# Hybrid decoder layer, S5 stage: one product with the B table, the state rotated ahead of one product with the C table, impulse-response products in four column groups

## The chip, the cores and the metric

The kernel runs on one core of one Trainium2 chip. The metric is the time of one execution on the device, in microseconds (us); lower is better. A core has five engines that matter here: TensorE (PE: products and transposes, the only one that writes sums to PSUM), VectorE (DVE), ScalarE (ACT), GpSimd (POOL) and SyncE (SP, which here only issues DMAs). Each engine takes its instructions in the order in which they were written to its queue; waits between engines go over semaphores.

## The reference

One decoder layer for a sequence of 1024 tokens with 1024 channels, all in float32: a token-mixing part with two branches (RWKV-7 and S5), merged by learned gates, an output projection, and a gated MLP with a short causal convolution. The change touches only the S5 branch, a diagonal complex state-space model over 32 groups of 16 channels with 64 complex states each:

```python
lam = lax.complex(a_re, a_im);  dt = jnp.exp(log_step)[:, None]
a_bar = jnp.exp(lam * dt)
b_bar = ((a_bar - 1.0) / lam)[..., None] * lax.complex(b_re, b_im)
bu = jnp.einsum('gpc,blgc->blgp', b_bar, ug)
_, states = lax.associative_scan(s5_combine, (a_elems, bu), axis=1)   # s_t = a_bar * s_(t-1) + bu_t
y = jnp.real(jnp.einsum('gcp,blgp->blgc', c, states)) + d * ug
y = jax.nn.gelu(y)
return y * jax.nn.sigmoid(y @ w_glu + b_glu)
```

## The kernel before

**Overall.** The front half of the kernel has three phases. First the norm and the projection of the S5 input u. Then the S5 stage. Then the RWKV stage, with merges and output projections. The MLP follows. Large products are made in three parts each (lines 172 to 174), since both operands are split into a high and a low float32r part; the three products for one block of 128 of the contracted dimension are one *step*, and eight steps make one 128 x 512 output of the input projection.

**S5 in blocks of eight tokens.** Eight tokens times 16 channels fill the 128 partitions, so a group's input is a 128 x 128 tile (`u8[b][:, g]`: one column for each block of eight tokens). A batch `b` is eight groups; there are four. Real parts of the 64 states lie in the partitions `HALF[0]` (0 to 63) and imaginary parts in `HALF[1]` (64 to 127). For a batch, `s5_tables` builds:
- `w` (lines 521 to 527), transposed on PE (546) and copied by ACT into `wT`: the B table, with a third block of 64 columns that is the negated first one (548);
- `ca`, the C table for nine powers (529 to 537), and `cb`, the same with its halves swapped and one negated (538, 539);
- `toep`, the direct part inside a block: products of B and C (`bb`, `ca`, line 555) give the impulse response, ACT copies it into `kpad` (556), DVE adds the skip term D (561), and eight DMAs spread it (564);
- `cs` and `sn`, cosines and sines of the rotation per block (566 to 577), and `ph`, the decay per block (578).

`s5_batch` then makes two sets of eight products with the B table, columns 0 to 127 and 64 to 191 of `wT` (599), so that the second set is the first one with its halves swapped and one of them negated. DVE rotates (602 to 604), scans over the blocks with real decay (605), and multiplies the scanned state `z` with `sn` and with `cs` (606, 607). Then come 24 products into one tile of PSUM: `toep` with u8, `ca` with `z*cs`, `cb` with `z*sn` (612 to 614). ACT copies the result out (615) and a DMA stores it in `YU` (616).

**What sets the order.** On PE the order is written out by a planner, `drive` (185). It has lanes, generators that emit PE instructions and yield a pair: the PE time of what they have emitted, and the time until their next part may run (or a condition). In the S5 stage there are two lanes, `s5_lane` for the batches and `tab_lane` for the tables; a batch needs its table, and table b needs batch b - 2. While no lane is due, or while the lanes have used more than their share of time (`PACE`, `CREDIT`), the planner emits *filler*: one step of the list `self.fill`, at 0.68 of its microseconds. Due times are constants (line 1907): `T_US` 5, `T_TAB` 20, `T_TRIG` 12, and `T_SCAN` 13 from the B products to the output products. The list holds the rest of the input projection (`mix_in`), the 16 gate tiles (`gate_tiles`), and later the merges (`merge`, `merge_s5`) and the output projection (`outproj`). When the S5 lanes are done, filler runs on until no accumulation is open (1834), and the RWKV lanes start (1848); the first half's outputs (`rwkv_out`, 924) put the merges on the list (1904). The other engines' queues are ordered by a scheduler of the language by priorities: filler above the S5 batches, these above the tables.

**Buffers.** The S5 products use the PSUM tile `chk` (two buffers), the filler `gm` (four buffers in the S5 stage, two in the RWKV stage). Tiles of 128 x 1024 that both functions share have the tag `T4` (eight buffers).

Of the kernel before, what the change touches and what calls it, by code (L numbers as in the profile page):

```python
# [9 lines left out]
F32 = mybir.dt.float32  # L10
# [3 lines left out]
ALU = mybir.AluOpType  # L14
# [11 lines left out]
HALF = (slice(0, 64), slice(64, 128))  # L26
# [40 lines left out]
class Kern:  # L67
# [425 lines left out]
    def s5_tables(self, b, d):  # L493

        nc, V, G, A = self.nc, self.nc.vector, self.nc.gpsimd, self.nc.scalar
        s, a = self.s5, self.a
        g8 = slice(b * 8, b * 8 + 8)
        mm = nc.tensor.matmul

        def bc_c(x):  # L500
            return x[:, g8].unsqueeze(2).to_broadcast([128, 8, 16])

        bre, bim, cre, cim = self.s5w[b]

# [24 lines left out]
        ca = self.s5p.tile([128, 8, 9, 16], F32, tag="ca", name=self.nm("ca"), bufs=2)  # L529
        ct = self.s5p.tile([128, 8, 9, 16], F32, tag="ct", name=self.nm("ct"))  # L530
        cb = self.s5p.tile([128, 8, 9, 16], F32, tag="cb", name=self.nm("cb"), bufs=2)
        def tab(eng, t, x, q, j0):
            eng.tensor_tensor(t[:, :, j0:9, :].rearrange("p g j c -> p j g c"), x.unsqueeze(1).to_broadcast([128, 9 - j0, 8, 16]),
                              q[:, j0:9, g8].unsqueeze(3).to_broadcast([128, 9 - j0, 8, 16]), ALU.mult)
        tab(V, ca, cre, s["q1"], 0)
        tab(V, ct, cim, s["q2"], 0)
        V.tensor_tensor(ca, ca, ct, ALU.add)
        A.copy(cb[HALF[0], :, 1:9, :], ca[HALF[1], :, 1:9, :])
        A.mul(cb[HALF[1], :, 1:9, :], ca[HALF[0], :, 1:9, :], -1.0)

        yield 0, T_TAB if b else T_TAB0

        wT = self.s5p.tile([128, 8, 3, 64], F32, tag="wT", name=self.nm("wT"))
        ps = self.chk().rearrange("p (g n) -> p g n", n=128)
        for g in range(8):
            nc.tensor.transpose(ps[:, g], w[:, g], self.cst("ident"))
        A.copy(wT[:, :, 0:2, :], ps.rearrange("p g (a n) -> p g a n", n=64))
        A.mul(wT[:, :, 2, :], ps[:, :, 0:64], -1.0)
        yield 1.0, 0

        kpad = self.s5p.tile([16, 8, 15, 16], F32, tag="kpad", name=self.nm("kpad"))
        G.memset(kpad[:, :, 0:7, :], 0.0)
        ps = self.chk().rearrange("p (g n) -> p g n", n=128)
        for g in range(8):
            mm(ps[0:16, g], bb[:, g, :], ca[:, g, 0:8, :], start=g % 4 == 0, stop=True, skip_group_check=True)
        A.copy(kpad[:, :, 7:15, :], ps[0:16].rearrange("p g (j c) -> p g j c", c=16))
        dg = self.s5p.tile([16, 8, 16], F32, tag="dg", name=self.nm("dg"))
        o, _ = CST["ident"]
        V.tensor_tensor(dg, self.csts[0:16, o:o + 16].unsqueeze(1).to_broadcast([16, 8, 16]),
                        s["d"][:, g8].unsqueeze(2).to_broadcast([16, 8, 16]), ALU.mult)  # L560
        V.tensor_tensor(kpad[:, :, 7, :], kpad[:, :, 7, :], dg, ALU.add)
        toep = self.t4(shape=(128, 8, 8, 16))
        for i in range(8):
            nc.sync.dma_start(toep[16 * i:16 * i + 16], kpad[:, :, i:i + 8, :])

        cs, sn, ph = self.t4(shape=(128, 8, 128)), self.t4(shape=(128, 8, 128)), self.t4(shape=(128, 8, 128))
        for t, f in ((ph, s["fh"]), (sn, s["fl"])):
            for g in range(8):
                A.activation(t[:, g], self.cst("nrow"), AF.Identity, scale=f[:, b * 8 + g:b * 8 + g + 1])
        V.tensor_scalar(cs, ph, MAGIC, -MAGIC, ALU.add, ALU.add)  # L570
        V.tensor_tensor(ph, ph, cs, ALU.subtract)
        V.tensor_tensor(ph, ph, sn, ALU.add)
        V.tensor_scalar(cs, ph, MAGIC, -MAGIC, ALU.add, ALU.add)
        V.tensor_tensor(ph, ph, cs, ALU.subtract)
        A.activation(cs, ph, AF.Abs)
        A.activation(sn, ph, AF.Sin, scale=SIN_SCALE)
        A.activation(cs, cs, AF.Sin, bias=self.hpi, scale=-SIN_SCALE)
        A.copy(ph, s["rho"][:, g8].unsqueeze(2).to_broadcast([128, 8, 128]))
        G.memset(ph[:, :, 0:1], 0.0)

        d.update(ca=ca, cb=cb, cs=cs, sn=sn, toep=toep, wT=wT, ph=ph)
        yield 1.8, T_TRIG

    def s5_batch(self, b, d, ys):

        nc, V, G, A = self.nc, self.nc.vector, self.nc.gpsimd, self.nc.scalar
        s = self.s5
        mm = nc.tensor.matmul
        ca, cb, cs, sn, toep, wT, ph = (d[n] for n in ("ca", "cb", "cs", "sn", "toep", "wT", "ph"))

        u8 = self.u8[b]
        z = self.t4(shape=(128, 8, 128))
        rot = self.t4(shape=(128, 8, 128))
        G.memset(rot[:, :, 0:1], 0.0)
        yield 0, T_US
        p1, p2 = (self.chk().rearrange("p (g n) -> p g n", n=128) for _ in range(2))
        for p, o in ((p1, 0), (p2, 1)):
            for g in range(8):
                mm(p[:, g], wT[:, g, o:o + 2, :], u8[:, g, :], start=g % 4 == 0, stop=True, skip_group_check=True)
        r2 = self.t4(shape=(128, 8, 128))  # L600
        lead, turn = (slice(None), slice(None), slice(0, 127)), rot[:, :, 1:128]
        V.tensor_tensor(turn, p1[lead], cs[lead], ALU.mult)
        V.tensor_tensor(r2[lead], p2[lead], sn[lead], ALU.mult)
        V.tensor_tensor(turn, turn, r2[lead], ALU.add)
        V.tensor_tensor_scan(*(t.rearrange("p g n -> p (g n)") for t in (z, ph, rot)), 0.0, ALU.mult, ALU.add)
        V.tensor_tensor(rot, z, sn, ALU.mult)
        V.tensor_tensor(z, z, cs, ALU.mult)
        y8 = self.t4(shape=(128, 8, 128))
        yield 3.6, T_SCAN
        ps = self.chk().rearrange("p (g n) -> p g n", n=128)  # L610
        for g in range(8):
            mm(ps[:, g], toep[:, g], u8[:, g, :], start=g % 4 == 0, stop=False, skip_group_check=True)
            mm(ps[:, g], ca[:, g, 1:9, :], z[:, g, :], start=False, stop=False, skip_group_check=True)
            mm(ps[:, g], cb[:, g, 1:9, :], rot[:, g, :], start=False, stop=True, skip_group_check=True)
        A.copy(y8, ps)
        nc.sync.dma_start(ys.rearrange("j c g n -> (j c) g n"), y8)
        yield 5.4, 0

# [1285 lines left out]
                self.fill += [self.merge(mg), self.merge_s5(self.first), self.outproj(0, mg, self.mx0)]  # L1904


T_US, T_TAB0, T_TAB, T_TRIG, T_SCAN = 5.0, 44.0, 20.0, 12.0, 13.0
T_LD, T_SQ, T_LT = 6.0, 3.0, 3.5
NEVA = 4
T_KN, T_BK, T_GR, T_NF, T_MT, T_INV, T_LV, T_CH = 7.0, 4.0, 4.0, 5.0, 8.0, 43.0, 1.0, 0.8  # L1910
# [86 lines left out]
```

## Time and profile before

| what | value |
|---|---|
| median of three runs | 1490.96 us (1488.9 to 1493.81) |
| span of the profiled execution (the page gives no other time for it) | 1491.1 us |
| PE busy, share of the span | 1435.8 us, 96% |
| PE weight loads | 1176.3 us, 79% |
| DVE busy | 1071.2 us, 72% |
| ACT busy | 729.8 us, 49% |
| first and last B product (line 599) | 131.0 and 241.6 us |
| last output product of S5 (line 614) starts | 260.6 us |

A busy time is the union of an engine's instructions; the ends of products are modelled, so what a set of products costs on PE is best read from the start of its first to the start of what follows. A row of the timeline gives start, duration, engine, line, operation, and in brackets the idle time before it with what ended it. A row of a table of stretches gives start and end, length, busy time and number of instructions for each engine, the granted clock of PE, and the DMA share and rate. A row of a group gives line, engine, operation, tiles, shapes and count, then busy time and the mean in ns, then idle time before it; where one line of the source is asked for, it gives shortest, median and longest in ns and the first and last start.

### The profile page before, as it was taken

The page shows a single profiled execution, that of the slowest core. Times are in us where ns is not written, and L with a number is a line of the kernel's source. Part 1 is how long each engine was busy: PE and PEld are TensorE (multiplying, and loading weights), DVE is VectorE, ACT ScalarE, POOL GpSimd, SP SyncE. Part 2 cuts the span into 40 slices and gives each one's busy share as a digit, 9 for nine tenths or more (in the row PEclk, how much of TensorE's full clock was granted, in tenths as well). Part 3 has the DMA queues.
Part 4 walks back from the last instruction along what each step waited for, and adds up shares of the span by engine and source line. Part 5 has one row for each costly group of instructions (what it writes and reads, how often), then busy time and mean ns, then how long its engine had stood idle before and what let it go on. Part 6 is the DMA issues. An engine that isn't in the chain of part 4 may idle for free. (4 is left out here: it accounts for less than half of the span.)

```text
span 1491.1 us, 24155 instructions
## 1 busy us (share of the span) xinstructions
PE 1435.8 (96%) x9284; PEld 1176.3 (79%) x9284; DVE 1071.2 (72%) x1761; ACT 729.8 (49%) x1167; POOL 58.9 (4%) x116
## 2 busy tenths in 40 slices
PE   7999999999999989899999999999999999999996
PEld 5778888778878778677878877888888887888785
DVE  8977765665325859646597798777777777697677
ACT  7677653443324553633554455444444444443351
POOL 0000000010100110100000000000000000000001
PEclk9999999999999999899999999999999999999998
DMA  6453433633511575733374643222222227934723
GB/s 217 121 194 116 129 94 91 212 113 122 164 59 58 171 226 163 189 109 108 121 222 150 205 127 121 85 85 85 85 85 81 76 70 260 328 125 133 236 83 113
DMA packets 121284, 206.26 MB, mean 138 GB/s; under 512 B 29248, under 2 KB 35520, under 8 KB 121168
## 3 DMA queue, kind: packets, MB, share of 16 engines
q1 hardware_dynamic: 113296, 182.43, 39.2%
q0 software_dynamic: 6144, 19.99, 4.0%
q10 hardware_dynamic: 1728, 2.29, 0.4%
q8 instruction: 73, 1.20, 0.4%
q14 instruction: 43, 0.35, 0.1%
HBM read 150.14 MB, written 52.43 MB: 136 GB/s over the span
## 5 line engine op out<-in xcount | busy, mean ns | idle before, releaser
L172 PE MATMUL gm<-hh,wh 128*128 128x512 f32 x672 | 277.0, 412 | 10.5 <-DVE ev L1192 4.3
L173 PE MATMUL gm<-hl,wh 128*128 128x512 f32 x672 | 265.4, 395 | 0.0
L174 PE MATMUL gm<-hh,wl 128*128 128x512 f32 x672 | 265.2, 395 | 0.0
L156 ACT CAST wh<-wf 128x512 fp32r<-128x512 f32 x171 | 105.6, 619 | 168.3 <-PE gm L173 103.8
L157 DVE TENSOR_TENSOR wl<-wf,wh 128x512 fp32r<-128x512 f32 x171 | 116.9, 686 | 77.6 <-ACT wh L156 77.3
L172 PEld LDWEIGHTS gm<-hh,wh 128*128 128x128 f32 x672 | 127.6, 190 | 42.8 <-issue 5.9
L174 PEld LDWEIGHTS gm<-hh,wl 128*128 128x128 f32 x672 | 128.0, 190 | 28.1
L173 PEld LDWEIGHTS gm<-hl,wh 128*128 128x128 f32 x672 | 128.2, 191 | 24.7 <-issue 1.0
L1615 PE MATMUL d<-xl,wh 128*128 128x512 f32 x308 | 121.4, 394 | 3.5 <-DVE xl L227 3.5
L1614 PE MATMUL d<-xh,wh 128*128 128x512 f32 x308 | 121.4, 394 | 2.1 <-ACT xh L226 2.1
L1616 PE MATMUL d<-xh,wl 128*128 128x512 f32 x308 | 121.2, 393 | 0.0
L1440 PE MATMUL rp<-t,h 128*128 128x512 f32 x216 | 84.4, 391 | 1.6 <-ACT p L1454 1.6
L1442 PE MATMUL rp<-t,l 128*128 128x512 f32 x216 | 84.2, 390 | 0.5 <-DVE l L227 0.5
L1441 PE MATMUL rp<-t,h 128*128 128x512 f32 x216 | 84.1, 389 | 0.0
L1615 PEld LDWEIGHTS d<-xl,wh 128*128 128x128 f32 x308 | 58.6, 190 | 16.5 <-DVE xl L227 4.3
L1614 PEld LDWEIGHTS d<-xh,wh 128*128 128x128 f32 x308 | 58.5, 190 | 14.8 <-ACT xh L226 2.5
L1616 PEld LDWEIGHTS d<-xh,wl 128*128 128x128 f32 x308 | 58.6, 190 | 12.2
L226 ACT CAST h<-r 128x1024 fp32r<-128x1024 f32 x34 | 35.8, 1054 | 61.1 <-PE rp L1441 29.6
L227 DVE TENSOR_TENSOR l<-r,h 128x1024 fp32r<-128x1024 f32 x34 | 41.6, 1224 | 29.2 <-ACT h L226 27.7
L1461 DVE SCALAR_TENSOR_TENSOR y<-zv,vecs,y 128x1023 f32<-128x1023 f32 (+1 forms) x36 | 46.1, 1280 | 8.5 <-ACT y L1459 8.5
L1440 PEld LDWEIGHTS rp<-t,h 128*128 128x128 f32 x216 | 40.5, 188 | 11.2 <-ACT p L1454 2.5
L1454 ACT COPY p<-rp 128x512 f32<-128x512 f32 x54 | 31.0, 574 | 36.5 <-PE rp L1442 36.5
(459 smaller groups left out, 3199.4 us busy)
## 6 DMA issues: line engine op xcount, KB each, us to landing
r<-in_w_up_dram SPq DMA_DIRECT2D x36, 512.0 KB, 3.7
wf<-in_w_in_dram SPq DMA_DIRECT2D x62, 256.0 KB, 3.1
st<-in_w_down_dram SPq DMA_DIRECT2D x55, 256.0 KB, 4.1
st<-ACT SPq DMA_DIRECT2D x44, 256.0 KB, 4.5
wf<-in_w_up_dram SPq DMA_DIRECT2D x36, 256.0 KB, 2.9
ACT<-y POOLq DMA_DIRECT2D x18, 512.0 KB, 2.9
GT<-ev SPq DMA_DIRECT2D x32, 256.0 KB, 2.6
wf<-in_w_br_dram SPq DMA_DIRECT2D x32, 256.0 KB, 2.9
```

Of the source, the lines that this page charges most:

```text
L156: nc.scalar.copy(h[:, :n], f[:, :n])
L157: nc.vector.tensor_tensor(l[:, :n], f[:, :n], h[:, :n].bitcast(F32), ALU.subtract)
L172: mm(ps, a, xh[k], start=k == 0, stop=False)
L173: mm(ps, a, xl[k], start=False, stop=False)
L174: mm(ps, b, xh[k], start=False, stop=k == n - 1)
L1440: mm(ps, wh[:, c], xh, start=first and k == 0, stop=False, skip_group_check=True)
L1441: mm(ps, wh[:, c], xl, start=False, stop=False, skip_group_check=True)
L1442: mm(ps, wl[:, c], xh, start=False, stop=k == 3, skip_group_check=True)
L1461: V.scalar_tensor_tensor(y[:, lag:], z[:, 0:1024 - lag], self.vec(nme, i), y[:, lag:], ALU.mult, ALU.add)
L1614: mm(ps, wh[:, c], xh[:, x], start=start, stop=False, skip_group_check=True)
L1615: mm(ps, wh[:, c], xl[:, x], start=False, stop=False, skip_group_check=True)
L1616: mm(ps, wl[:, c], xh[:, x], start=False, stop=stop, skip_group_check=True)
```

## The change

- **B products once.** `wT` loses its third block, and `s5_batch` makes one set of eight products. The swapped and partly negated copy that the second set gave is made by ACT from the first set, half by half (`A.copy`, `A.mul` into `r2`), and DVE multiplies it with `sn` in place.
- **The state rotated.** The table `cb` goes. After the scan, ACT writes the state with its halves swapped and one negated into `rot`; DVE forms `z*cs`, `rot*sn` and their sum; one product with `ca` takes the place of two. With the halves swapped in the state, not in the table, the sum over 128 partitions is the same.
- **Impulse response in four column groups.** The eight products with 16 result rows go to PSUM partitions 0, 32, 64 and 96 instead of all to 0, two products each, in two banks. Four ACT copies bring them into `kpad` instead of one.
- **The planner's numbers.** The yields of the products become 1.8 and 3.6 instead of 3.6 and 5.4 in `s5_batch`, and 0.9 instead of 1.0 for the transposes in `s5_tables`; the 1.8 after the impulse-response products stays. `T_SCAN` becomes 18 instead of 13.

```diff
 # s5_tables
         V.tensor_tensor(ca, ca, ct, ALU.add)
-        A.copy(cb[HALF[0], :, 1:9, :], ca[HALF[1], :, 1:9, :])
-        A.mul(cb[HALF[1], :, 1:9, :], ca[HALF[0], :, 1:9, :], -1.0)
...
-        wT = self.s5p.tile([128, 8, 3, 64], F32, tag="wT", name=self.nm("wT"))
+        wT = self.s5p.tile([128, 8, 128], F32, tag="wT", name=self.nm("wT"))
...
-        A.copy(wT[:, :, 0:2, :], ps.rearrange("p g (a n) -> p g a n", n=64))
-        A.mul(wT[:, :, 2, :], ps[:, :, 0:64], -1.0)
-        yield 1.0, 0
+        A.copy(wT, ps)
+        yield 0.9, 0
...
         for g in range(8):
-            mm(ps[0:16, g], bb[:, g, :], ca[:, g, 0:8, :], start=g % 4 == 0, stop=True, skip_group_check=True)
-        A.copy(kpad[:, :, 7:15, :], ps[0:16].rearrange("p g (j c) -> p g j c", c=16))
+            q = 32 * (g % 4)
+            mm(ps[q:q + 16, g // 4 * 4], bb[:, g, :], ca[:, g, 0:8, :], start=True, stop=True, skip_group_check=True)
+        for q in range(4):
+            A.copy(kpad[:, q::4, 7:15, :], ps[32 * q:32 * q + 16, 0::4].rearrange("p g (j c) -> p g j c", c=16))
...
 # s5_batch
-        p1, p2 = (self.chk().rearrange("p (g n) -> p g n", n=128) for _ in range(2))
-        for p, o in ((p1, 0), (p2, 1)):
-            for g in range(8):
-                mm(p[:, g], wT[:, g, o:o + 2, :], u8[:, g, :], start=g % 4 == 0, stop=True, skip_group_check=True)
+        p1 = self.chk().rearrange("p (g n) -> p g n", n=128)
+        for g in range(8):
+            mm(p1[:, g], wT[:, g], u8[:, g, :], start=g % 4 == 0, stop=True, skip_group_check=True)
         r2 = self.t4(shape=(128, 8, 128))
         lead, turn = (slice(None), slice(None), slice(0, 127)), rot[:, :, 1:128]
+        A.copy(r2[HALF[0]], p1[HALF[1]])
+        A.mul(r2[HALF[1]], p1[HALF[0]], -1.0)
         V.tensor_tensor(turn, p1[lead], cs[lead], ALU.mult)
-        V.tensor_tensor(r2[lead], p2[lead], sn[lead], ALU.mult)
+        V.tensor_tensor(r2, r2, sn, ALU.mult)
         V.tensor_tensor(turn, turn, r2[lead], ALU.add)
         V.tensor_tensor_scan(*(t.rearrange("p g n -> p (g n)") for t in (z, ph, rot)), 0.0, ALU.mult, ALU.add)
-        V.tensor_tensor(rot, z, sn, ALU.mult)
+        A.mul(rot[HALF[0]], z[HALF[1]], -1.0)
+        A.copy(rot[HALF[1]], z[HALF[0]])
         V.tensor_tensor(z, z, cs, ALU.mult)
+        V.tensor_tensor(rot, rot, sn, ALU.mult)
+        V.tensor_tensor(z, z, rot, ALU.add)
         y8 = self.t4(shape=(128, 8, 128))
-        yield 3.6, T_SCAN
+        yield 1.8, T_SCAN
         ps = self.chk().rearrange("p (g n) -> p g n", n=128)
         for g in range(8):
             mm(ps[:, g], toep[:, g], u8[:, g, :], start=g % 4 == 0, stop=False, skip_group_check=True)
-            mm(ps[:, g], ca[:, g, 1:9, :], z[:, g, :], start=False, stop=False, skip_group_check=True)
-            mm(ps[:, g], cb[:, g, 1:9, :], rot[:, g, :], start=False, stop=True, skip_group_check=True)
+            mm(ps[:, g], ca[:, g, 1:9, :], z[:, g, :], start=False, stop=True, skip_group_check=True)
...
-        yield 5.4, 0
+        yield 3.6, 0
...
-T_US, T_TAB0, T_TAB, T_TRIG, T_SCAN = 5.0, 44.0, 20.0, 12.0, 13.0
+T_US, T_TAB0, T_TAB, T_TRIG, T_SCAN = 5.0, 44.0, 20.0, 12.0, 18.0
```

More of the change, by code (lines that the diff above doesn't have):

```diff
@@ L530, in s5_tables @@
         ct = self.s5p.tile([128, 8, 9, 16], F32, tag="ct", name=self.nm("ct"))
-        cb = self.s5p.tile([128, 8, 9, 16], F32, tag="cb", name=self.nm("cb"), bufs=2)
         def tab(eng, t, x, q, j0):
@@ L579, in s5_tables @@
         G.memset(ph[:, :, 0:1], 0.0)
-        d.update(ca=ca, cb=cb, cs=cs, sn=sn, toep=toep, wT=wT, ph=ph)
+        d.update(ca=ca, cs=cs, sn=sn, toep=toep, wT=wT, ph=ph)
         yield 1.8, T_TRIG
@@ L588, in s5_batch @@
         mm = nc.tensor.matmul
-        ca, cb, cs, sn, toep, wT, ph = (d[n] for n in ("ca", "cb", "cs", "sn", "toep", "wT", "ph"))
+        ca, cs, sn, toep, wT, ph = (d[n] for n in ("ca", "cs", "sn", "toep", "wT", "ph"))
         u8 = self.u8[b]
```

## The prediction

> **What bounds the kernel now.** I read the page first, then the busy time of each engine over the stretch in which the changed lines run, then what TensorE (PE) waits for.
>
> ```profile
> span 1491.1 us, 24155 instructions
> PE 1435.8 (96%) x9284; PEld 1176.3 (79%) x9284; DVE 1071.2 (72%) x1761; ACT 729.8 (49%) x1167; POOL 58.9 (4%) x116
> ```
>
> ```profile
> core 0: us, PE busy (x) PEld busy (x) DVE busy (x) ACT busy (x) POOL busy (x), PEclk, DMA share, GB/s
> 107.00:262.00 155.00, 155.00 (x891) 133.93 (x890) 101.75 (x135) 90.36 (x162) 3.30 (x10) 1.00 0.36 111
> ```
>
> The S5 stage (tables and batches of `s5_tables` and `s5_batch`, 107 to 262 us) leaves PE not one idle microsecond: 155.00 of 155.00 at full clock. Its chains on VectorE (DVE) and ScalarE (ACT) are hidden behind filler products of the input projection. So PE work that is taken away here should come off the time one for one, if two things hold: the chains still fit behind the filler, and the filler that moves forward isn't missed later. The sum is made on the span, 1491.1 us; it stands 0.1 us above the median of the runs, 1490.96, so I carry it over as it is.
>
> **What PE loses.** The next rows show three stretches of PE: the products with the B table of one batch, the output products of one batch, and the impulse-response products of one table, with the transposes ahead of them; then the groups' counts over all four batches.
>
> ```profile
> core 0: us, PE busy (x), PEclk, DMA share, GB/s
> 131.00:134.49 3.49, 3.49 (x33) 1.00 0.11 17
> 149.77:155.04 5.27, 5.27 (x49) 1.00 0.34 50
> 147.12:148.97 1.85, 1.85 (x17) 1.00 0.39 148
> 146.16 1.03 PE L546 MATMUL chk<-csts,t 128*128 128x128 f32 x8
> ```
>
> ```profile
> L614 PE MATMUL chk<-t,cb 128*128 128x128 f32 x64 | 12.4, 275 | 0.0
> L555 PE MATMUL chk<-ca,sml 128*16 128x128 f32 x64 | 7.7, 273 | 0.0
> ```
>
> Line 599 makes the 8 products of a batch twice; one set goes: 3.49 / 2 = 1.75 us. Of the three sets of lines 612 to 614 the third goes (64 records, 16 a batch, each product being two records): 5.27 / 3 = 1.76 us. Together 3.5 us a batch, **14.0 us** over four.
>
> The impulse-response products (16 records a table, 16 columns wide) take 1.85 us one behind the other, 0.116 us a record. No row shows four column groups with all 128 rows. The nearest is line 716, which uses two row halves and two column halves:
>
> ```profile
> 292.20 1.98 PE L716 MATMUL cz<-ar,bk 64*64 64x128 f32 x64
> ```
>
> Here 64 records of the same 128 streamed columns take 1.98 us, 0.031 us each: nearly four at once, though each half of the rows is shared by two column halves. At that rate 16 records take 0.5 us; with no overlap they stay at 1.85. I take 0.6, near the first end, because line 716 couldn't come near a factor of four with row halves alone. That is 1.25 us a table, **5.0 us** in all. The bounds are 0 and 5.4. PE loses 19.0 us.
>
> **What ACT and DVE gain.**
>
> ```profile
> L538 ACT COPY cb<-ca x4: 1045/1048/1050, 97.8 to 197.6; 64x1024 f32<-64x1024 f32 x4
> L548 ACT ACTIVATE wT<-chk x4: 603/603/603, 112.3 to 219.6; 128x512 f32<-128x512 f32 x4
> L556 ACT COPY kpad<-chk x4: 1002/1002/1003, 113.3 to 220.6; 16x1024 f32<-16x1024 f32 x4
> L756 ACT COPY bk<-cz 64x256 f32<-64x256 f32 x32 | 11.7, 367 | 0.5
> L607 DVE TENSOR_TENSOR t<-t,t x4: 1215/1218/1225, 145.8 to 249.3; 128x1024 f32<-128x1024 f32 x4
> ```
>
> ACT drops both halves of the swapped C table (2 x 1.05), the negated third of wT (0.60) and one kpad copy (1.00): 3.7 us a batch. It adds four half swaps of the size of line 538, two out of PSUM and two of the state (4.2), and four kpad copies of 256 elements, by line 756 0.37 each (1.5): 5.7. DVE adds one pass of 1.22. That is +2.0 and +1.2 us a batch, hidden as amounts of work, since ACT is busy 90 and DVE 102 of 155 us. What counts is where they stand: all four swaps and the added pass lie on the chain from the B products to the state, which PE waits for in order, with all filler behind it.
>
> **Does the chain still fit?** The planner's filler steps are three products each; line 172 is the first of each three, so its counts are steps.
>
> ```profile
> 134.40:146.10 11.70, 6.70 (x17) 1.00 0.20 69
> 148.90:149.70 0.80, 0.50 (x1) 1.00 0.43 159
> 241.60:255.30 13.70, 7.87 (x20) 1.00 0.18 60
> 260.50:266.20 5.70, 3.20 (x8) 1.00 0.30 110
> 526.00:556.00 30.00, 12.40 (x30) 1.00 0.79 234
> 721.50:737.50 16.00, 9.04 (x23) 1.00 0.45 148
> ```
>
> A step takes 11.70 / 17 = 0.69 us and the planner counts 0.68. Between the B products and the outputs of a batch lie 17 + 1 = 18 steps and one table's transposes and impulse products. With T_SCAN at 18 the planner must reach 18: 23 steps (15.64) and the table's 0.9 + 1.8. The gap on PE becomes 23 x 0.69 + 1.0 + 0.6 = 17.4 us. Now the first batch and the second, in order of time:
>
> ```profile
> 136.20 1.22 DVE L602 TENSOR_TENSOR t<-chk,t 128x1016 f32<-128x1016 f32 x1 [0.36 <-ACT t L577]
> 141.57 2.28 DVE L605 TENSOR_TENSOR_SCAN t<-t,t 128x1024 f32<-128x1024 f32 x1
> 145.83 1.22 DVE L607 TENSOR_TENSOR t<-t,t 128x1024 f32<-128x1024 f32 x1
> 149.99 0.39 PE L613 MATMUL chk<-t,ca 128*128 128x128 f32 x2
> 180.18 1.22 DVE L607 TENSOR_TENSOR t<-t,t 128x1024 f32<-128x1024 f32 x1
> 185.71 0.39 PE L613 MATMUL chk<-t,ca 128*128 128x128 f32 x2
> ```
>
> In the first batch DVE does not wait for PE but for the cosine table of line 577, which ACT finishes at 136.2; two swaps ahead of it in ACT's queue push it by 2.1. The state is then ready at 147.05 + 2.1 + 2.1 (swaps after the scan) + 1.2 = 152.5. PE, whose B products now end at 131.0 - 1.25 + 1.75 = 131.5, asks for it at 131.5 + 17.4 + 0.2 = 149.1. So PE waits about **3.4 us** in the first batch (bounds: 0, if the swaps slip into ACT's idle gaps, and 5). The second batch has 185.71 - 181.40 = 4.3 us of slack; its gap grows by 17.4 - (18 x 0.69 + 1.0 + 1.85 = 15.3) = 2.1 and its chain by up to 5.4, so it ends 1.0 to the good; I put **0.5 us** on batches two to four.
>
> A wait can cost PE a second time, by the clock:
>
> ```profile
> 500.00:520.00 20.00, 16.95 (x89) 0.83 0.49 134
> 540.00:560.00 20.00, 15.82 (x73) 0.92 0.77 220
> 557.34 0.79 PE L172 MATMUL gm<-hh,wh 128*128 128x512 f32 x1 [2.70 <-ACT ev L1147]
> ```
>
> A granted clock of 0.92 over 20 us is 20 x 0.08 / 0.5 = 3.2 us at half speed, in the slice with the 2.70 us wait; 0.83 is 6.8 us. So a new 3.4 us wait likely brings 3.4 us at half speed: **1.7 us** more (bounds 0 and 3.4). The Trainium skill ("TensorE: Matmul & The Clock Gate", What's actually happening) has the gate close only after a whole idle window of about 3.4 us; by it this term would mostly be 0 and the forecast 1.7 lower, but the trace's 2.70 us wait had the low clock beside it.
>
> **Where the filler goes.** The tables' due times are unchanged, so the stage keeps its length in the planner's time and the removed products are replaced by filler. From the first B products to the end of the stage there are now 3 x (18 + 17) + 20 + 8 = 133 steps (17 again between outputs and the next B products); afterwards 3 x (23 + 17) + 27 + 2 = 149, because draining stops at the next end of an eight-step accumulation. Sixteen steps, 10.9 us, are thus done in S5 and missing later. Rows of the later places:
>
> ```profile
> PE gm L172 <- ACT ev L1147: 4.2, 2, 2.7
> 525.76 0.60 PE L924 MATMUL rp<-csts,mt 128*128 128x128 f32 x4
> 532.36 0.80 PE L172 MATMUL gm<-hh,wh 128*128 128x512 f32 x1
> L226 ACT CAST hh<-ld x4: 619/622/623, 533.3 to 540.0; 128x512 fp32r<-128x512 f32 x4
> 721.25 0.60 PE L924 MATMUL rp<-csts,mt 128*128 128x128 f32 x4
> 725.35 0.69 DVE L227 TENSOR_TENSOR e<-ld,e 128x512 fp32r<-128x512 f32 x1
> ```
>
> The RWKV stage begins at 266.2 + 10.9 - 19.0 + 5.6 = 263.7, 2.5 us earlier. After its first output lane (last transpose 525.76) there were 30 steps, the last four of them the first merge product. Of the 26 gate steps 10 remain: four ran before the lanes' own products, the fifth starts at 532.36, and six more end at 532.4 + 6 x 0.69 = 536.5, so merging now starts at 536.5 - 2.5 = 534 and its fourth step at 536, while the last of the four stored outputs it reads is split at 540.0 + 0.6 + 0.7 - 2.5 = 538.8: a wait of 2.8. I add 2 for the gate loads behind it on SyncE's queue. The two waits of 4.2 us that gate evictions caused there, stuck behind the GELUs on ACT, go, as the gates are through before the GELUs. Net **0.6 us**. After the second output lane 23 steps of output projection were left; 7 remain. The next merge's fourth step comes at 721.25 + 0.4 + 10 x 0.69 = 728.5 and its last input is split at 726.0: covered. I put **0.5 us** on the change of pools there.
>
> **The sum.** -19.0 + 3.4 + 0.5 + 1.7 + 0.6 + 0.5 = -12.3 us: 1491.1 - 12.3 = 1478.8, which I call **1478.5 us**, 0.8% faster.
>
> **The rivals.**
> - *Everything comes off.* The swaps fall into ACT's gaps, PE never waits in S5, and the merge waits that go balance those that come: 1491.1 - 19.0 = 1472. For it: ACT is idle 65 of 155 us. Against: the first batch is already late by its cosine table.
> - *The column groups do not overlap*, so the change doesn't do what it says in that part: 5.0 us stay, 1478.5 + 5.0 = 1483.5. For it: all eight products use the same 128 rows, which line 716 never does. Against: that line's factor. By the Trainium skill ("TensorE: Matmul & The Clock Gate", The mechanism) weight loads overlap running products only where row groups differ, which speaks for this rival; the same page (Measured speedup vs the span model) lists a measured 2.38 for three column groups, which speaks against it. No run here shows it yet.
> - *The cover is missed later.* All sixteen steps come back as PE waits around the merges: 1491.1 - 19.0 + 5.6 + 10.9 = 1488.6, no measurable change. For it: lanes there run on latency, and only 7 steps are left after the second output lane. Against: the inputs' times above.
> - *The state is late in every batch: slower.* ACT takes its instructions in order; if the swaps queue behind table work each time, PE stands at line 613 with all filler behind it. It costs more than it brings once each batch loses 19.0 / 4 = 4.8 us. With 4.5 us late and 1.7 us of half clock: 4 x 6.2 = 24.8, 1491.1 - 19.0 + 24.8 = 1497. For it: the chain has 5.4 us more against 2.1 us more gap. Against: later batches had over 4 us of slack.
>
> **How the numbers follow.** Forecast 0.50, everything 0.15, no overlap 0.10, missed cover 0.16, late state 0.09. A difference under 0.3% (4.5 us) can't be told from none here. The first three are faster: 0.75; missed cover is no change: 0.16; late state is slower: 0.09. The range goes from 1469 (everything, and the low clock around 557 us gone: 19.0 + 1.6, and a little) to 1489.5, just past the missed cover; only the late state and a little of the first lie outside.
>
> **What would show it.** Right: 8 products a batch at line 599's successor in 1.75 us; outputs in 3.5; impulse products in 0.6; 23 steps between B products and outputs; one PE wait of some 3 us at the first state, with a clock under 1.00 near it; RWKV starting 2 to 3 us sooner; no gate-eviction wait near 557. Wrong: PE waits at every batch's state (late state), 1.85 us impulse products (no overlap), or new PE waits adding up to 10 us between 530 and 630 or after 720 (missed cover).

## The result and the profile after

The changed kernel takes 1504.86 us (median; 1502.67 to 1510.48) where the kernel before takes 1490.06 (1488.9 to 1493.81) beside it: ratio 1.0109, interval 1.0084 to 1.0134. It is slower by 1.1%. The profiled execution has a span of 1504.7 us against 1491.1, so 13.6 us are to be found.

First the page of the changed kernel, then the busy time of the engines over its S5 stage (columns: length of the stretch, then busy time and instructions of each engine, granted clock, DMA share, GB/s).

```profile
span 1504.7 us, 23918 instructions
PE 1427.6 (95%) x9156; PEld 1163.4 (77%) x9156; DVE 1074.8 (71%) x1765; ACT 738.1 (49%) x1183; POOL 59.1 (4%) x116
```

```profile
107.00:269.40 162.40, 154.94 (x829) 130.51 (x827) 108.41 (x145) 104.55 (x186) 3.31 (x10) 0.98 0.37 112
```

Before, PE had no idle time in S5 (155.00 of 155.00, clock 1.00). Now it stands 7.5 of 162.4 us, and the clock is 0.98. The work itself went down as the change says. PE alone over one batch's products with the B table, its output products, and one table's impulse responses:

```profile
129.73:131.43 1.70, 1.70 (x17) 1.00 0.50 96
229.08:232.57 3.49, 3.49 (x34) 1.00 0.52 128
111.36:111.92 0.56, 0.56 (x18) 1.00 0.80 300
```

These were 3.49, 5.27 and 1.85: per batch 1.79 + 1.78 + 1.29 us less, 19.4 in all. So some 33 us came back elsewhere. The next two fences cut both kernels, before and then changed, at the same five places: start of RWKV's transposes, last group of transposes of the first half's outputs, first transpose of the second half's chain behind the first merge, last group of transposes of the second half's outputs, and the products of line 245 behind the first four steps of the second merge. They show line 172 alone, so the count in brackets is the number of filler and merge steps in the stretch.

```profile
100.00:277.80 177.80, 74.44 (x188) 1.00 0.41 126
525.76:611.60 85.84, 41.13 (x98) 0.94 0.67 196
721.25:741.06 19.81, 10.71 (x27) 1.00 0.38 122
```

```profile
100.00:286.37 186.37, 81.69 (x204) 0.96 0.41 126
534.78:630.40 95.62, 42.01 (x98) 0.93 0.64 187
739.07:756.54 17.47, 5.49 (x11) 0.72 0.55 178
```

| stretch | before | after | difference | by work and steps alone | lost |
|---|---|---|---|---|---|
| S5 and the step to RWKV | 177.80 | 186.37 | +8.6 | -19.0 + 16 x 0.69 = -8.0 | 16.6 |
| first RWKV half | 247.96 | 248.41 | +0.4 | 0 | 0.4 |
| first merge | 85.84 | 95.62 | +9.8 | 0 | 9.8 |
| second half's chain | 109.65 | 108.67 | -1.0 | 0 | -1.0 |
| to the second merge | 19.81 | 17.47 | -2.3 | -16 x 0.69 = -11.0 | 8.7 |
| the rest | 750.04 | 748.16 | -1.9 | 0 | -1.9 |

The sixteen steps are where the prediction put them: 16 more before RWKV, 16 fewer before the second merge. The waits of PE over 1 us in the changed kernel's S5 stage, at the step to RWKV and ahead of the second merge, from its timeline (start, duration, instruction, in brackets the idle time before it and what ended it):

```profile
150.29 0.49 PE L613 MATMUL chk<-u,t 128*128 128x128 f32 x2 [1.28 <-ACT wT L543]
153.07 0.80 PE L614 MATMUL chk<-t,ca 128*128 128x128 f32 x2 [2.29 <-DVE t L608]
...
193.27 0.49 PE L614 MATMUL chk<-t,ca 128*128 128x128 f32 x2 [3.79 <-DVE t L608]
...
274.64 0.77 PE L172 MATMUL gm<-hh,wh 128*128 128x512 f32 x1 [5.15 <-DVE last L1075]
...
751.26 0.79 PE L172 MATMUL mm<-e,wh 128*128 128x512 f32 x1 [6.80 <-ACT wh L156]
```

The first three are S5's own, 7.4 us. The first of them is not yet a wait for the state: PE lacks a PSUM buffer, which the transposes of the next table hold until ACT copies them out (line 543), and in ACT's queue that copy stands behind the swaps of the scanned state (604, 605):

```profile
147.63 1.05 ACT L605 COPY t<-t 64x1024 f32<-64x1024 f32 x1
...
149.23 1.01 ACT L543 COPY wT<-chk 128x1024 f32<-128x1024 f32 x1
```

PE would have stood for the state of that batch anyway, until 153.0, so I count both waits as its lateness. The fourth wait stands at the step to RWKV and the fifth at the second merge. In the kernel before, the same two places show:

```profile
268.17 0.47 PE L172 MATMUL gm<-hh,wh 128*128 128x512 f32 x1 [1.84 <-DVE last L1075]
...
738.20 0.50 PE L172 MATMUL mm<-e,wh 128*128 128x512 f32 x1 [0.68 <-ACT mx L1316]
```

In the changed kernel PE ran at a lower clock near each of these waits:

```profile
140.00:160.00 20.00, 16.43 (x98) 0.91 0.29 89
180.00:200.00 20.00, 16.11 (x96) 0.91 0.24 68
260.00:280.00 20.00, 14.85 (x73) 0.83 0.39 131
740.00:760.00 20.00, 13.20 (x51) 0.74 0.53 169
```

### The profile page after: what moved, and what is told of

It reads as the page before. It is cut to its first block, busy times and chain, and to the rows that moved or that the text cites. A ratio compares the mean times of both kernels' runs of the same rounds, so it can differ in the third digit from the quotient of the medians.

```text
span 1504.7 us, 23918 instructions
## 1 busy us (share of the span) xinstructions
PE 1427.6 (95%) x9156; PEld 1163.4 (77%) x9156; DVE 1074.8 (71%) x1765; ACT 738.1 (49%) x1183; POOL 59.1 (4%) x116
## 3 DMA queue, kind: packets, MB, share of 16 engines
q10 hardware_dynamic: 1728, 2.29, 0.4%
```

## The experiments

My theory (A): PE work counts one for one, and what was lost is time in which PE waits, because the S5 states and buffers come late and because filler pulled into S5 is missing as cover later. The rival (B): the work moved to ACT and DVE costs time in any order.

**Column groups alone**, on the kernel before, planner's numbers as before:

```diff
-            mm(ps[0:16, g], bb[:, g, :], ca[:, g, 0:8, :], start=g % 4 == 0, stop=True, skip_group_check=True)
-        A.copy(kpad[:, :, 7:15, :], ps[0:16].rearrange("p g (j c) -> p g j c", c=16))
+            q = 32 * (g % 4)
+            mm(ps[q:q + 16, g // 4 * 4], bb[:, g, :], ca[:, g, 0:8, :], start=True, stop=True, skip_group_check=True)
+        for q in range(4):
+            A.copy(kpad[:, q::4, 7:15, :], ps[32 * q:32 * q + 16, 0::4].rearrange("p g (j c) -> p g j c", c=16))
```

> The kernel before with the column groups alone; every yield and T_SCAN as before, so the order on PE is the same. Theory A (work counts one for one, what the whole change lost comes from filler moved forward and from late states): PE loses 4 x 1.29 us (the changed kernel shows 0.56 against 1.85 a table), no step moves, no state is late (the first had 2.9 us of slack, the gap shrinks by 1.29): 1490 - 5 = 1485, interval below 1. Theory B (the stages are bound by their lanes, PE is only filled up; work taken from PE comes back as waits): 1490, no change.

Measured: 1483.79 us (1482.81 to 1489.17), ratio 0.997 (0.9954 to 0.9986) to the 1489.07 of the kernel before beside it: 5.3 us faster for 5 us of PE work.

**The planner's numbers alone**, on the kernel before (all its products stay):

```diff
-        yield 1.0, 0
+        yield 0.9, 0
...
-        yield 3.6, T_SCAN
+        yield 1.8, T_SCAN
...
-        yield 5.4, 0
+        yield 3.6, 0
...
-T_US, T_TAB0, T_TAB, T_TRIG, T_SCAN = 5.0, 44.0, 20.0, 12.0, 13.0
+T_US, T_TAB0, T_TAB, T_TRIG, T_SCAN = 5.0, 44.0, 20.0, 12.0, 18.0
```

> The kernel before with only the planner's numbers of the change (yields 1.8, 3.6, 0.9 and T_SCAN 18): the same work, and in S5 sixteen filler steps more, as in the changed kernel. Theory A: no state waits in S5; the wait at the start of the RWKV stage 5 us as in the changed kernel instead of 1.8, new waits at the first merge and about 7 us at the second: what the changed kernel lost outside S5, 13.6 + 19.0 - 10.8 (its state waits of 7.4 and their low clock of 3.4) = 21.8, so 1490 + 22 = 1512. Rival (what was lost outside S5 comes from the changed ACT and DVE work, not from the order): 1490, no change.

Measured: 1514.57 us (1510.02 to 1519.04), ratio 1.0173 (1.0148 to 1.0199): 25.5 us slower with the same work on every engine. Its longest waits of PE (in all, times, longest):

```profile
PE gm L172 <- DVE ev L1192: 7.2, 2, 4.2
...
PE mm L172 <- ACT wh L156: 6.7, 1, 6.7
PE gm L172 <- DVE last L1075: 5.1, 1, 5.1
PE gm L172 <- DVE hl L1192: 3.3, 2, 2.1
```

There is no wait at a state, and the waits at RWKV's start and at the second merge are those of the changed kernel. So they come from the order, not from ACT's or DVE's new work.

**The change with the planner's numbers of before** (the four edits above, undone):

> The changed kernel with the planner's numbers of before (yields 3.6, 5.4, 1.0 and T_SCAN 13): the same steps between the same lanes as in the kernel before. Theory A: nothing new after S5 (1.8 us at the start of RWKV, no 6.8 us wait at the second merge); in S5 every state is late, as the gap is 18 steps: by some 7.5, 7.5, 3 and 3 us, 21 in all, with a low clock of 1.7 each: 1490 - 19 + 21 + 7 = 1499. Rival (the loss outside S5 comes from the changed work): 1499 + 22 = 1521.

Measured: 1497.82 us (1496.16 to 1501.21), ratio 1.0064 (1.0049 to 1.0079). The waits change places:

```profile
PE chk L614 <- DVE t L608: 8.9, 4, 2.7
PE chk L613 <- ACT wT L543: 8.5, 3, 4.2
```

With 18 steps of cover every batch is late, and the second merge waits 0.7 again. The 8.5 us are waits for the PSUM buffer of line 543, whose copy again stands behind the swaps of the state; the state itself comes later still.

**The change without the four half swaps**, so that its S5 branch computes something else:

```diff
-        A.copy(r2[HALF[0]], p1[HALF[1]])
-        A.mul(r2[HALF[1]], p1[HALF[0]], -1.0)
...
-        V.tensor_tensor(r2, r2, sn, ALU.mult)
+        V.tensor_tensor(r2[lead], p1[lead], sn[lead], ALU.mult)
...
-        A.mul(rot[HALF[0]], z[HALF[1]], -1.0)
-        A.copy(rot[HALF[1]], z[HALF[0]])
+        V.tensor_tensor(rot, z, sn, ALU.mult)
...
-        V.tensor_tensor(rot, rot, sn, ALU.mult)
```

> The changed kernel without its four half swaps a batch on ACT: the products with sn read the B product and the state unswapped, so the S5 branch computes something else; everything else, the order on PE too, is the changed kernel's. Theory A: the two state waits of 3.6 and 3.8 us and the low clock after them go, the loss outside S5 stays: 1505 - 11 = 1494. Rival (late states cause the later losses too, by shifting the lanes against the filler): 1490 - 19 = 1472.

Measured: 1494.12 us (1488.44 to 1499.73), ratio 1.0023 (1.0005 to 1.0041); waits at the states 0.2 us in all, the later ones (5.2, 6.8, 7.1) still there. These four agree: the order alone +25.5, the work -19, together +6.5 against +5.1 measured without the swaps (interval 0.7 to 6.1); the swaps, with the late states that they cause, add some 11.

**A better order for the change.** In the changed kernel's first three batches DVE waits for the sine table (line 573) ahead of line 601. Its timeline in the second batch, on ACT:

```profile
171.59 1.02 ACT L598 COPY t<-chk 64x1024 f32<-64x1024 f32 x1 [1.20 <-PE chk L595]
172.62 1.02 ACT L599 ACTIVATE t<-chk 64x1024 f32<-64x1024 f32 x1
173.66 1.06 ACT L572 ACTIVATE t<-t 128x1024 f32<-128x1024 f32 x1
...
176.83 1.28 ACT L573 ACT_TABLE_LOAD   x1
178.13 1.06 ACT L573 ACTIVATE t<-t 128x1024 f32<-128x1024 f32 x1
```

The swaps (2.0 us) stand in ACT's queue ahead of the absolute value and the sine, which in turn gate the chain. Casts and evictions of the filler, 2.2 us from 174.63 on, follow between the absolute value and the load of the sine table; in the kernel before that load followed at once. So I gave the sines more time and the tables ahead of them less, to keep the stage's length:

```diff
-T_US, T_TAB0, T_TAB, T_TRIG, T_SCAN = 5.0, 44.0, 20.0, 12.0, 18.0
+T_US, T_TAB0, T_TAB, T_TRIG, T_SCAN = 5.0, 38.0, 12.0, 16.0, 18.0
```

> The change whole, with four numbers of the planner set anew: first tables 38 instead of 44, later tables 12 instead of 20, sines 16 instead of 12, scan 18 as in the change. A replay of the planner's arithmetic gives 23 steps between B products and outputs as in the change, 32 and 27 steps (26 and 21) between impulse responses and B products, and 219 steps to the end of the stage where the kernel before has 220 and the change 240. Theory A (the 19 us of TensorE work count one for one; what was lost on top is the state that comes late because the sines are late and the swaps lengthen its chain, and the filler that is missing as cover later): state waits under 1 us in all, the wait at the start of RWKV back to about 1.8 us, the 6.8 us wait at the second merge back under 1 us, 1470 us (1467 to 1477). Rival B (the swaps on ScalarE cost time in any order, because they delay evictions and casts): 1485 us or more, with the waits spread over many lines.

Measured: 1480.54 us (1474.38 to 1483.83), ratio 0.9942 (0.9924 to 0.996) to 1488.73: **faster than both kernels**, 24 us below the change with the same instructions on PE. The time lies between the two expectations. The wait at the second merge is 0.68 and that at RWKV's start 2.01. But more than half of the 19 us is still missing, in S5:

```profile
107.00:253.50 146.50, 139.73 (x750) 118.05 (x749) 105.51 (x139) 102.27 (x183) 3.70 (x10) 0.98 0.37 117
138.98 0.41 PE L551 MATMUL chk<-ca,sml 128*16 128x128 f32 x8 [3.15 <-DVE t L600]
...
174.69 0.63 PE L551 MATMUL chk<-ca,sml 128*16 128x128 f32 x8 [2.92 <-ACT wT L543]
```

The next batch's tables now come so early that their impulse products find both PSUM buffers (`chk`, two of them) taken: one still read by line 600, one by the copy of line 543.

**More time for the sines alone** (T_TRIG 16 instead of 12 in the change, nothing else):

> The change with one number of the planner altered: sines 16 instead of 12, so that the B products come 5 to 6 steps later after the tables in every batch, and the stage takes some 24 more steps of filler than the change (264 against 240 by the replay). Theory A: the state waits of S5 (7.4 us in the change) fall under 1.5 us, because the sines no longer end after the B products; what is saved there is paid later by the missing filler (wait at the start of RWKV 5 us or more, second merge 6 us or more), 1500 to 1512 us. Rival (the swaps alone make the state late, not the sines): state waits stay at 6 us or more.

Measured: 1523.19 us (1519.25 to 1525.23), ratio 1.023 (1.0204 to 1.0256). The waits of S5's output products fell from 7.4 to 4.3 us, between the two expectations, so the sines explain a part of the lateness. The time misses theory A's range: the missing filler cost more than I expected. Here 227 steps stand before RWKV (204 in the change), and at the first merge PE waits 8.1 us for the split of one input.

**Column groups and the B products once**, the C products left double, in the order of before. On top of the first experiment (with it go the third block of `wT` and the product with `sn`, as in the change):

```diff
-        for p, o in ((p1, 0), (p2, 1)):
-            for g in range(8):
-                mm(p[:, g], wT[:, g, o:o + 2, :], u8[:, g, :], start=g % 4 == 0, stop=True, skip_group_check=True)
+        for g in range(8):
+            mm(p1[:, g], wT[:, g], u8[:, g, :], start=g % 4 == 0, stop=True, skip_group_check=True)
...
+        A.copy(r2[HALF[0]], p1[HALF[1]])
+        A.mul(r2[HALF[1]], p1[HALF[0]], -1.0)
```

> The kernel before with two of the three parts, and its own order: column groups, and the B products once with their swapped halves by ScalarE; the C products stay two, with the second table of C, and the planner keeps the numbers of before. TensorE work falls by 4 x (1.25 + 1.75) = 12 us. Theory A: the two swaps of the B products lengthen the state's chain by about 2 us; with 17 steps between B products and outputs and 1.6 us to spare in the first batch without swaps that leaves waits of 0 to 3 us in all, 1479 us (1476 to 1485). Rival B (each swap costs in any order): 1484 us or more, no better than column groups alone.

Measured: 1485.6 us (1482.14 to 1491.55), ratio 0.9983 (0.9968 to 0.9998). That is no better than the column groups alone: the rival's outcome, and just outside theory A's range. The state waits are larger than I allowed for, 5.6 us against 3, and they would explain it under theory A too, so this run does not decide between the two:

```profile
PE chk L614 <- DVE t L608: 5.6, 2, 3.9
```

**Less cover in S5, more behind it**: the retuned kernel with other numbers.

```diff
-T_US, T_TAB0, T_TAB, T_TRIG, T_SCAN = 5.0, 38.0, 12.0, 16.0, 18.0
+T_US, T_TAB0, T_TAB, T_TRIG, T_SCAN = 5.0, 36.0, 12.0, 16.0, 16.0
```

> The change whole, with first tables 36, later tables 12, sines 16 and scan 16: 20 steps between B products and outputs, 213 steps to the end of the stage. Theory A: with the sines in time, 20 steps (about 13.6 us) of cover against a chain of about 13 to 15 us leave state waits of 0 to 5 us in all; 1473 us (1468 to 1481), near the retuned kernel with 23 steps. If it is faster than that one, the filler is worth more behind the stage than in it; if it is slower by more than its state waits, it is worth less. Rival B: 1485 us or more.

Measured: 1496.54 us (1492.55 to 1499.66), ratio 1.0053 (1.0035 to 1.007). Theory A's range is missed by far. The time lies in the rival's open range, but the swaps are not all of it: state and buffer waits in S5 are 5.8 and 3.4 us, RWKV's start waits 4.1, and the second merge waits 5.38 us although 35 steps stand in the stretch ahead of it, more than the 27 of the kernel before. The last of these breaks the reading "cover is missing at the second merge".

**The same order with more distance between the tables and the B products ahead of them:**

```diff
-T_US, T_TAB0, T_TAB, T_TRIG, T_SCAN = 5.0, 38.0, 12.0, 16.0, 18.0
+T_US, T_TAB0, T_TAB, T_TRIG, T_SCAN = 5.0, 35.0, 16.0, 14.0, 18.0
```

> The change whole, with first tables 35, later tables 16, sines 14, scan 18. In the retuned kernel with tables 12 TensorE waited 3.15 and 2.92 us at the impulse responses of the next batch, for PSUM buffers that the B products (read by DVE) and the transposes (read by ACT) still held; there 7 steps lay between B products and the next tables. Here it is 13 by the replay, 10 between those tables and the outputs, 23 between B products and outputs, and 221 steps in the stage (220 before, 240 in the change). Theory A (every late buffer and state counts one for one, and the order alone decides them): these two waits fall under 1 us together, no state wait over 1 us, and the time is 1489 - 19 = 1470 to 1476 us. Rival B (part of the gain of 19 us is lost to ScalarE's swaps in any order): 1479 us or more, though the waits are gone.

Measured: 1482.91 us (1480.39 to 1484.16), ratio 0.9939 (0.9915 to 0.9963) to 1490.38. The PSUM waits went (0.4 us left), and a state wait came back:

```profile
PE chk L614 <- DVE t L608: 5.4, 2, 4.6
```

With sines 14 the second batch's sine is late again (DVE waits 3.97 us for it). The gain is that of the first retuned kernel. The time misses theory A's range and lies in the rival's, but the rival's condition, that the waits are gone, was not reached, so this run leaves it open.

**What holds up the second merge?** In the changed kernel, SyncE's queue waited 8.8 us at loads of x (line 1287) that stand between two weight blocks of that merge:

```profile
SPq L1287 <- DVE e L227: 8.8, 1, 8.8
```

So I issued those loads on GpSimd's queue:

```diff
-            nc.sync.dma_start(xs[k], resid(k, o))
+            (nc.sync if th or squares is None else nc.gpsimd).dma_start(xs[k], resid(k, o))
```

> The change, with the eight loads of x for the norm after the second merge issued on GpSimd's queue instead of SyncE's; no other instruction is moved. In the change six of these loads stand on SyncE's queue between the second and the third weight block of the second merge, and wait there 8.8 us for buffers that the last split of the RWKV output holds; the weights behind them land late, and TensorE waits 6.80 us. If that queue is the cause: this wait falls under 2 us, everything before 740 us stays as in the change, and the time is 1498 us (1496 to 1501). Rival (the cover alone: with 11 steps of filler left the weights cannot be there in time): the wait stays at 5 us or more and the time at 1503 us or more.

Measured: 1508.48 us (1506.11 to 1509.25), ratio 1.011 (1.0081 to 1.0138), no faster than the change; the wait grew to 9.25 us. These loads are not the cause. With x out of the way, SyncE waits for something else:

```profile
SPq L155 <- DVE et L1323: 12.1, 1, 12.1
```

In the changed kernel itself the rows stand in a chain behind the last output-projection step:

```profile
744.49 0.59 ACT L1316 COPY mx<-gm 128x512 f32<-128x512 f32 x1 [1.87 <-PE gm L174]
745.11 0.63 ACT L1321 ACTIVATE ev<-mx 128x512 f32<-128x512 f32 x1
745.77 0.69 DVE L1323 TENSOR_TENSOR et<-ev,ev 128x512 f32<-128x512 f32 x1 [2.42 <-ACT ev L1321]
746.50 0.80 SPq L155 DMA_DIRECT2D wf<-in_w_br_dram  x2
750.59 0.62 ACT L156 CAST wh<-wf 128x512 fp32r<-128x512 f32 x1 [4.85 <-DMA wf<-in_w_br_dram]
```

The load of a weight block is issued when the squares of the last output tile are summed; only then is it cast, and PE starts. This chain begins with the last filler step, so no amount of filler ahead of it helps. Why only in some orders? Raw weight blocks (`wf`) go round a ring of four slots, two in the weights' pool and two in RWKV's, but of two slots before RWKV starts. Following the counter of `load_w` through the code, the ring widens at the 30th block in the kernel before, at the 32nd in the change and at the 28th with scan 16. The first block of the second merge then falls into slot 0 in the first case and into slot 2 in the two others. For that merge the slots 2 and 3 lie in a pool of their own (`wfx`, in `mix_out`), which is opened when RWKV's pools are closed. The next two kernels move the counter only, in the change and in the kernel with scan 16:

```diff
-            self.wfp = self.rk
+            self.wfp, self.wfs = self.rk, 3
```

> The change, with the ring of raw weight blocks set two slots further where RWKV starts (no work and no TensorE order changed). In the kernel before and in both retuned kernels the first weight block of the second merge falls into slot 0 of that ring (the pool of the weights), in the change, where RWKV starts two blocks later, and in the retuned kernel with scan 16, where it starts two blocks sooner, into slot 2 (the pool of RWKV); there the load was issued only when the squares of the last output projection tile were done, and TensorE waited 6.80 and 5.38 us. If the slot is the cause: that wait falls to 0.7 us as before though only 11 steps of filler are left, everything up to 740 us stays within 1 to 2 us of the change, and the time is 1504 - 6 to 8 = 1497 us (1495 to 1499). Rival (cover): the wait stays at 5 us or more, 1503 us or more.

> The retuned kernel with scan 16 (213 steps, 35 steps of filler left for the stretch before the second merge), with the same edit to the ring of raw weight blocks. If the slot is the cause: the wait of 5.38 us at the second merge falls to 0.7 us and the time from 1496.5 to 1490 us (1487 to 1492). Rival (cover, or something else in that order): the wait stays at 4 us or more, 1494 us or more.

Measured, for the change: the wait is gone with 11 steps ahead of it, as expected,

```profile
748.52 0.50 PE L172 MATMUL mm<-e,wh 128*128 128x512 f32 x1 [0.68 <-ACT mx L1316]
```

and the stretch to the second merge went from 17.47 to 8.9 us. But the time is 1502.17 us (1501.04 to 1502.88), ratio 1.0089 (1.0064 to 1.0114), not 1497, because the first merge's stretch grew by 3.3 us to 98.9; the edit moves every block from the start of RWKV on, and whether that is why was not tried. Measured with scan 16: 1484.86 us (1480.75 to 1488.5), ratio 0.9972 (0.9958 to 0.9987) to 1488.88, against 1496.54 without the edit; the wait fell from 5.38 to 0.68:

```profile
730.51 0.50 PE L172 MATMUL mm<-e,wh 128*128 128x512 f32 x1 [0.68 <-ACT mx L1316]
```

The slot is the cause of this wait. The time fell by more than I expected (1487 to 1492): of the 11 us between the two profiles 6.9 lie in the stretch to the second merge, the rest in small pieces elsewhere, 2.0 of them ahead of RWKV's transposes; what made those is open.

## Why the prediction was wrong

The forecast was 1478.5 us, faster, with 1489.5 as the upper end. The result lies on the other side. The step that failed is "Where the filler goes". I counted the sixteen moved steps rightly, but priced their move at 0.6 + 0.5 us and the step to RWKV at nothing. The move alone, with the old work, costs 25.5 us; in the change 3.3 of waiting were added at that step, 9.8 were lost at the first merge and 8.7 on the way to the second. A second term was too small, the 0.5 us for the states of batches two to four. Point by point:

- **What PE loses: right.** 19.4 us measured for 19.0. The column groups overlap (0.56 us a table for a predicted 0.6; the rival "no overlap" is dead). The retuned kernels, the same work in another order, run 1480.5 to 1482.9.
- **Where the filler goes: the count was right, its price was not.** Sixteen steps moved from the stretch ahead of the second merge into S5. The three places where that cost time are the step to RWKV and the two merges, below.
- **First state: right.** Predicted wait 3.4; measured 1.28 + 2.29 = 3.6, the 1.28 at the PSUM buffer, which I had not foreseen. PE asks for the state at 150.8 and gets it at 153.0 (predicted 149.1 and 152.5).
- **Second state: mis-sized.** I let its chain grow by up to 5.4 us and put 0.5 us on batches two to four. From the first B product to the finished state it took 14.7 us before (166.7 to 181.4) and 23.6 after (169.6 to 193.2): +8.9. The growth that I allowed has 2.1 us for swaps ahead of the table. In the second batch the sine table ends 9.6 us after the B products start, where it had ended 4.5 us after: 5.1 later, as the filler's casts and evictions came between, too. The third and fourth chains grew by 5.0 and 6.0, and there PE did not wait.
- **Low clock: too small.** I had 1.7 us for one wait. There were slices of 0.91, 0.91 and 0.83 in S5 and at its end, and 0.74 at the second merge. The three of S5 are worth 20 x (0.09 + 0.09 + 0.17) = 7.0 us at full speed, the part inside the waits included.
- **The step to RWKV: not priced.** I let RWKV start 2.5 us sooner; it starts 8.6 us later (286.37 against 277.80). Of the S5 stretch's 16.6 us, 7.4 are state waits, 3.3 the longer wait at the step (5.15 for 1.84), and the rest about what the low clock takes. RWKV's buffers take the place of S5's, and here the store of the last batch stands in the way. Its copy on ACT, before and then after:

```profile
260.91 1.01 ACT L615 COPY t<-chk 128x1024 f32<-128x1024 f32 x1 [4.67 <-PE chk L614]
```

```profile
268.15 1.02 ACT L615 COPY t<-chk 128x1024 f32<-128x1024 f32 x1 [6.96 <-PE chk L614]
272.10 0.69 ACT L1072 ACTIVATE ev<-gm,mu 128x512 f32<-128x512 f32 x1 [2.93 <-DMA YU<-t]
```

Eight filler steps stood behind the last output products before and two stand there now, so the 3 us in which the result lands in memory are open. I had counted these 8 and 2 myself and drawn nothing from them.

- **First merge: mis-sized.** I had 0.6 net: an input that comes late by 2.8, 2 for the loads of gates behind it, and 4.2 of gate evictions that go. The late input is there (1.8 us in the changed kernel, at the split of line 226), and the evictions of gate tiles (line 1147) fell from 4.2 to 2.0. What I had not priced are the waits for the merge's own gate products (line 1192), 9.5 us where 3.0 stood. Before and then after:

```profile
L172 PE MATMUL gm<-hh,wh 128*128 128x512 f32 x98 | 41.1, 420 | 7.2 <-ACT ev L1147 4.2 <-DVE ev L1192 3.0
```

```profile
L172 PE MATMUL gm<-hh,wh 128*128 128x512 f32 x98 | 42.0, 429 | 13.5 <-DVE ev L1192 7.1 <-DVE hl L1192 2.4 <-ACT ev L1147 2.0
```

PE is idle 6.6 us longer in this stretch; the other 3.2 are products that run slower. The stretch holds 98 steps either way, but in the change 16 steps of gate tiles have left it for S5, and 16 steps from further along the list have come in. Its length follows the order and hardly the work: 95.6 to 98.9 us in the five kernels with 203 or 204 steps before RWKV in the trace, 82.5 to 85.8 in the six with 186 to 189, 78 in the two with 180. Which load or eviction in it is first late wasn't tried.
- **Second merge: wrong.** I looked at the merge's last input (ready in time) and called it covered. PE waited 6.80 us for its first weight block, whose slot in a ring depends on how many blocks were loaded before RWKV started. In the profile of before the wait was 0.68, since there the first block fell into the other slot.

Of the rivals, "the cover is missed later" came nearest, but its 10.9 us were no upper bound: what was lost behind S5 isn't limited by the length of the filler that left, and the wait at the second merge is no missing cover at all, since it goes with 11 steps of filler when the slot is another. "The state is late in every batch" happens when the change keeps the order of before (17.4 us of waits in four batches, 8.5 of them at the PSUM buffer); with the change's own numbers two of four were late. That ACT's and DVE's added work makes the change slower in any order is refuted by the same instructions running in 1480.5 us. That a part of the gain is lost to it in any order is not: the B products once and the two later retuned kernels came out in that rival's range, each with waits of its own.

Still open: some 11 us between the best order found (8.2 us faster by the medians) and the full 19. In the first and the last retuned kernel 6 to 7 of them stand as waits in S5, with low clock beside them, with the sines and the two PSUM buffers pulling the same numbers in opposite directions.

## What to carry to other kernels

When a schedule fills an engine with work from a shared list, price a change as two edits: what it removes, and where the list's end moves; run the second alone, since here it cost 25.5 us, more than the 19 that the change takes off PE. Moving work onto an in-order engine delays whatever stands behind it in each round, so follow the whole queue in every batch, not only in the one with the least slack. Where a wait appears that no missing cover explains, follow it back through the queue to the buffer: a ring that falls into another phase cost 6 us of waiting here with no work changed.

## What the runs showed of the hardware

- **Four column groups of 16 columns** with all 128 rows run nearly at once: 1.85 us became 0.56 for eight float32 products, a factor of 3.3. The Trainium skill ("TensorE: Matmul & The Clock Gate", Measured speedup vs the span model) lists 2.38 for three groups; the trace agrees in kind and adds the fourth.
- **A low clock came with some waits of 1.8 to 3.2 us, and not with others.** In the retuned kernel the waits of 3.15 us (at 138.98) and 2.92 us (at 174.69) stand beside these slices:

```profile
140.00:160.00 20.00, 19.30 (x95) 0.91 0.39 122
160.00:180.00 20.00, 17.08 (x96) 0.91 0.29 95
```

The same wait of 1.84 us at the start of RWKV has a clock of 1.00 in the kernel before and of 0.91 with the column groups alone:

```profile
260.00:280.00 20.00, 18.16 (x92) 1.00 0.66 215
```

```profile
260.00:280.00 20.00, 18.16 (x81) 0.91 0.74 230
```

By the Trainium skill (same page, What's actually happening) PE falls back after a whole idle window of some 3.4 us; these waits are shorter, so the measurement decides: a low clock stood beside some of them. What decides between the two rows isn't settled by any run here.
